# Up-projections of a hybrid decoder trunk in pairs of strips, seven block products for eight

## The chip, the cores and the metric

The kernel runs on one core of one Trainium2 chip. Its time is the device time of one execution in microseconds (us). A core has TensorE (PE, the matrix engine, whose weight loads are listed as PEld), VectorE (DVE), ScalarE (ACT), GpSimd (POOL) and SyncE (SP, which issues the DMAs here). Each takes its instructions in an order fixed when the program is built, and waits on semaphores for the others.

## The reference, cut to what matters

A trunk of two layers on 528 tokens (512 and 16 learned ones ahead) of 1024 channels. Layer 0 mixes tokens with a gated delta net, layer 1 with a short gated convolution; each mixer is followed by a gated FFN, and each of the four sub-layers ends in a layer norm. The change lies in the second, third and fourth sub-layer:

```python
def short_conv_mixer(h, w_in, conv_w, w_out):
    b_gate, c_gate, xv = jnp.split(h @ w_in, 3, axis=-1)     # w_in 1024 x 3072
    u = causal_dwconv(c_gate * xv, conv_w)
    return (b_gate * u) @ w_out

def conv_ffn(h, w_up, conv_w, w_down):
    u, gate = jnp.split(h @ w_up, 2, axis=-1)                # w_up 1024 x 5632
    u = causal_dwconv(u, conv_w)                             # width 3
    return (jax.nn.silu(u) * gate) @ w_down                  # w_down 2816 x 1024

# per layer: h <- layer_norm(ALPHA * h + mixer(h)); h <- layer_norm(ALPHA * h + conv_ffn(h))
```

## The kernel before, in words

Activations lie with channels on the 128 partitions: `h` is [128, 8 blocks of channels, 528 tokens] in fp32. Every product is made in three matmuls with operands split in a high and a low part: `split` (L71 to L73) lets ACT write the high part (L72) and DVE the rest, `lo = src - hi` (L73). `hh` and `hl` are the parts of `h`, `gh` and `gl` those of the gated middle, `whi` and `wlo` those of a weight strip. A strip is the weights of 128 output channels, [128, 8 blocks, 128], 512 KB.

`mm_steps` (L169) runs over the blocks k of a strip and issues high x high (L174), high x low (L175) and low x high (L176) into one PSUM bank. `prep` (L137) loads a strip on SP's queue into one of four raw buffers and splits it; `get` (L153) keeps up to five strips prepared ahead, in ten buffers of a strip each (NW, L129; four of them in the delta net).

The delta net comes first; then for each sub-layer `up` (L688) and `down` (L636). [...] It begins with a lead of six strips whose first halves all go before any second half, so that PE has work while the norm of the second half of the tokens is still being made. `emit` takes the bank: for u a copy on ACT, three taps on DVE (`conv3`, L724), Silu on ACT; for a gate a product on DVE and a split into `gh` and `gl` (`gated`, L732). The FFN's 22 strips of the middle go in groups of 8, 8 and 6 (THIRDS, L103), and after each group `down` adds its part of the second product to `h` (L651, L653). The last `down` of a sub-layer holds back the second halves of five or seven strips, makes the norm of the first half (`lnorm`, L592) beside them, then theirs.

What stands in which order on an engine is decided when the program is built, by a scheduler that goes by its own costs; the code's order is its priority. The banks of `up` and `down` are six (`pm`).

## Time and profile before

| what | us |
|---|---|
| time, median of 3 runs (lowest, highest) | 1389.57 (1387.96, 1390.41) |
| the profiled execution: span from first to last instruction | 1386.2 |
| delta net | 0 to about 378 |
| its output projection and first norms | 378 to about 422 |
| first FFN | 422 to about 805 |
| short convolution | 805 to about 990 |
| second FFN, with the end | 990 to 1386 |
| HBM read and written over the span | 112.05 MB and 2.10 MB, 82 GB/s |

The stages are told apart by where the means of the norms are computed (two each, at 414, 795, 983 and 1354 us for the first of them). Rows of a timeline give start and length in us, then engine, line and operation, output and inputs, shapes and how many were merged; the bracket at the end is the idle time of that engine just before, and what ended it. A row of the groups gives busy us and mean ns of one, then the idle time before it.

### The profile page before, as it was taken

To read this page: it belongs to the slowest core of one execution; us is meant where nothing else is said; L and a number is where in the kernel's file an instruction comes from. 1 tells how busy PE (TensorE), PEld (TensorE's weight loads), DVE (VectorE), ACT (ScalarE), POOL (GpSimd) and SP (SyncE) were. 2 spreads that over 40 slices of the span, in tenths; PEclk is the share of its full clock that TensorE was granted. 3 is DMA by queue.
4 is the path that set the end of the run, shared out by engine and by line. 5 is a ranking of instruction groups with operands and counts; after the bars stand their busy time and mean duration, and the time that the engine had idled before them with its cause. 6 is when DMAs were issued, how large, how long until landed. Compare 5 with 4: busy or idle time off the path is not lost.

```text
span 1386.2 us, 25494 instructions
## 1 busy us (share of the span) xinstructions
PE 1350.4 (97%) x10769; PEld 1288.0 (93%) x10769; DVE 804.9 (58%) x1360; ACT 606.2 (44%) x1218; POOL 90.1 (7%) x132
## 2 busy tenths in 40 slices
PE   8999999999999999999999999999999999999996
PEld 7888998988899999999999999999999889988996
DVE  6767767766469754455344496444775434443436
ACT  6677777676446532233223274222463223322314
POOL 0323322221000000000000000000000000000000
PEclk9999999999999999999999999999999999999999
DMA  5211111211272433233322233333124333322101
GB/s 193 66 58 32 47 32 31 62 32 35 74 244 77 123 93 93 92 94 94 95 79 80 61 107 122 92 92 92 51 87 138 93 97 99 92 92 80 58 1 61
DMA packets 34929, 115.78 MB, mean 84 GB/s; under 512 B 3840, under 2 KB 6400, under 8 KB 34816
## 3 DMA queue, kind: packets, MB, share of 16 engines
q1 hardware_dynamic: 34176, 112.04, 26.3%
q0 software_dynamic: 640, 2.12, 0.4%
q8 instruction: 84, 1.38, 0.4%
q14 instruction: 29, 0.24, 0.1%
HBM read 112.05 MB, written 2.10 MB: 82 GB/s over the span
## 4 chain that ended last, share of the span: by engine, by line
PE 87%; DVE 5%; ACT 4%; issue 2%; POOL 1%; DMA 0%; SPq 0%; ACTq 0%; POOLq 0%; DVEq 0%
PE pu L174 15%; PE pu L175 15%; PE pu L176 15%; PE pd L175 8%; PE pd L174 8%; PE pd L176 8%; PE ps L175 2%; PE ps L174 2%; PE ps L176 2%; DVE acc L316 1%; DVE wlo L73 1%; PE psz L176 1%; PE psz L175 1%; PE psz L174 1%; PE p L403 1%
## 5 line engine op out<-in xcount | busy, mean ns | idle before, releaser
L174 PE MATMUL pu<-hh,whi 128*128 128x258 f32 (+3 forms) x1632 | 477.6, 294 | 1.4 <-ACT hh L632 1.4
L175 PE MATMUL pu<-hl,whi 128*128 128x258 f32 (+3 forms) x1632 | 478.3, 293 | 0.0
L176 PE MATMUL pu<-hh,wlo 128*128 128x258 f32 (+3 forms) x1632 | 477.2, 293 | 0.0
L72 ACT ACTIVATE whi<-raw 128x1024 fp32r<-128x1024 f32 (+2 forms) x209 | 216.7, 1040 | 387.8 <-PE pu L175 168.1
L73 DVE TENSOR_TENSOR wlo<-raw,whi 128x1024 fp32r<-128x1024 f32 (+2 forms) x209 | 249.6, 1196 | 227.0 <-ACT whi L72 224.3
L174 PEld LDWEIGHTS pu<-hh,whi 128*128 128x128 f32 x1632 | 306.8, 188 | 9.1 <-ACT hh L632 1.8
L175 PEld LDWEIGHTS pu<-hl,whi 128*128 128x128 f32 x1632 | 307.3, 188 | 7.5 <-DVE hl L633 0.2
L176 PEld LDWEIGHTS pu<-hh,wlo 128*128 128x128 f32 x1632 | 307.6, 189 | 7.0
L174 PE MATMUL pd<-gh,whi 128*128 128x256 f32 (+3 forms) x704 | 213.4, 303 | 0.0
L175 PE MATMUL pd<-gl,whi 128*128 128x256 f32 (+3 forms) x704 | 212.9, 302 | 0.0
L176 PE MATMUL pd<-gh,wlo 128*128 128x256 f32 (+3 forms) x704 | 212.7, 302 | 0.0
L174 PEld LDWEIGHTS pd<-gh,whi 128*128 128x128 f32 x704 | 132.8, 189 | 5.8
L175 PEld LDWEIGHTS pd<-gl,whi 128*128 128x128 f32 x704 | 132.6, 188 | 5.8
L176 PEld LDWEIGHTS pd<-gh,wlo 128*128 128x128 f32 x704 | 132.7, 188 | 5.7
L174 PE MATMUL ps<-hh,whi 128*128 128x264 f32 x384 | 114.1, 298 | 2.1 <-ACT acc L313 2.1
L176 PE MATMUL ps<-hh,wlo 128*128 128x264 f32 x384 | 115.1, 300 | 0.0
L175 PE MATMUL ps<-hl,whi 128*128 128x264 f32 x384 | 114.6, 298 | 0.0
L174 PEld LDWEIGHTS ps<-hh,whi 128*128 128x128 f32 x384 | 73.4, 191 | 2.6 <-ACT acc L313 2.5
L756 ACT ACTIVATE c<-c 128x516 f32<-128x516 f32 (+1 forms) x44 | 27.6, 632 | 106.8 <-DVE c L727 106.8
L175 PEld LDWEIGHTS ps<-hl,whi 128*128 128x128 f32 x384 | 73.4, 191 | 0.4
L176 PEld LDWEIGHTS ps<-hh,wlo 128*128 128x128 f32 x384 | 73.3, 191 | 0.2 <-DVE wlo L73 0.2
L316 DVE SCALAR_TENSOR_TENSOR acc<-cb,par_sb,acc 128x528 f32<-128x528 f32 x72 | 59.0, 820 | 20.0 <-ACT acc L313 19.6
(228 smaller groups left out, 1865.1 us busy)
## 6 DMA issues: line engine op xcount, KB each, us to landing
raw<-in_w_up_dram SPq DMA_DIRECT2D x88, 512.0 KB, 3.6
raw<-in_w_dn_dram SPq DMA_DIRECT2D x32, 512.0 KB, 3.5
raw<-in_w_bi_dram SPq DMA_DIRECT2D x24, 512.0 KB, 3.6
raw<-in_w_qkv_dram SPq DMA_DIRECT2D x23, 512.0 KB, 3.7
raw<-in_w_dn_dram SPq DMA_DIRECT2D x16, 384.0 KB, 3.1
raw<-in_w_z_dram SPq DMA_DIRECT2D x8, 512.0 KB, 3.6
raw<-in_w_ao_dram SPq DMA_DIRECT2D x8, 512.0 KB, 3.6
raw<-in_w_bo_dram SPq DMA_DIRECT2D x8, 512.0 KB, 3.5
```

What stands on the lines that cost most here:

```text
L72: S.activation(hi, src, AF.Copy)
L73: V.tensor_tensor(lo, src, hi.bitcast(F32), ALU.subtract)
L174: TE.matmul(ps, hi[:, k, :], r_h, start=start and k == 0, stop=False)
L175: TE.matmul(ps, hi[:, k, :], r_l, start=False, stop=False)
L176: TE.matmul(ps, lo[:, k, :], r_h, start=False, stop=stop and k == nk - 1)
L316: V.scalar_tensor_tensor(acc, cb[:, t_ : t_ + T], par_sb[:, wo + t_ : wo + t_ + 1], acc, ALU.mult, ALU.add)
L403: TE.matmul(p1[:CH, c, :CH], N16[:, c, :], r_, start=True, stop=True)
L756: S.activation(c, c, AF.Silu)
```

## The change

Two strips and both halves of the tokens make a 2 x 2 block product: the two strips are cut at half of the channels (A11, A12 of the first, A21, A22 of the second), the tokens likewise in channels and at half of the tokens. Instead of eight block products of four blocks k each there are seven, by the scheme of Strassen in Winograd's form: four weight sums (S1 = A21 + A22, S2 = S1 + A11, S3 = A21 + A11, S4 = S2 + A12, signs put into the token sums and into negated taps), and four token sums made once for a sub-layer (`sums_a`, `sums_b`). In the code a product is called by its weight block. A product has 4 x 3 matmuls of n = 260 columns (first FFN) or 258; a pair has 84 matmuls.

The FFN's groups become 4, 6, 6 and 6: the first is made as before (eight strips, the first six as the lead), the other 18 pairs of gate and u strip as pairs. The short convolution makes two columns of strips as before, then a `down` of two blocks, then eight pairs, and a `down` of six. Weights lie in a ring of 32 + 24 blocks for high and low parts (`room`, `done`) instead of ten strips; `pump` loads and splits what fits, also at the very start. `conv3` of a pair makes its first tap on ACT.

```diff
+GROUPS = ((0, 4), (4, 6), (10, 6), (16, 6))
+SC_GROUPS = ((0, 2), (2, 6))
+PREP = ("A11", "S1", "S2", "A12", "S3", "A22", "S4")
-    THIRDS = ((0, 8), (8, 8), (16, 6))
...
+    SEG = (32, 24)
+    def room(n):
+        g_, p_ = state["seg"], state["pos"]
+        if p_ + n > SEG[g_]:
+            g_, p_ = (g_ + 1) % len(segs), 0
+        for u in live:
+            if u.seg == g_ and u.pos < p_ + n and p_ < u.pos + u.n:
+                return None
...
+    def sums(job, what):
+        a, b = job.raws
+        a11, a12, a21, a22 = a[:, 0:4, :], a[:, 4:8, :], b[:, 0:4, :], b[:, 4:8, :]
+        if what == "S1":
+            job.s = pools[-1].tile([P, 4, P], F32, name=f"s{job.n}", tag="s", bufs=1)
+            V.tensor_tensor(job.s, a21, a22, ALU.add)
+        elif what == "S2":
+            V.tensor_tensor(job.s, job.s, a11, ALU.add)
+        elif what == "S3":
+            V.tensor_tensor(a21, a21, a11, ALU.add)
+        elif what == "S4":
+            V.tensor_tensor(job.s, job.s, a12, ALU.add)
...
+    def pump(end=None):
+        while True:
+            i = state["load"]
+            if i < len(jobs) and i < (n_gdn + 4 if len(pools) == 1 else len(jobs)) \
+                    and state["held"] + len(jobs[i].srcs) <= 2 * len(pools):
+                jobs[i].n = i
+                load(jobs[i])
+                state["load"] += 1
+                continue
+            i = state["prep"]
+            if i >= state["load"] or (end is not None and i >= end):
+                return
+            if not prep_step(jobs[i]):
+                return
...
-    prep(0)
+    pump(1)
     for k in range(1, KD):
         nc.sync.dma_start(h[:, k, :], xt[:, k, :])
...
+    def sums_a(sb):
+        n, B = blocks(sb)
+        for q in (0, 2):
+            ks = slice(q, q + 2)
+            t3 = tmp("c", f"t3_{sb}_{state['use']}_{q}")[:, : 2 * n].rearrange("p (k t) -> p k t", k=2)
+            V.tensor_tensor(t3, B(h, 1, 1)[:, ks], B(h, 0, 1)[:, ks], ALU.subtract)
+            V.scalar_tensor_tensor(sc[:, ks, :n], t3, -1.0, B(h, 0, 0)[:, ks], ALU.mult, ALU.subtract)
+            split(sumh[:, 1, ks, :n], suml[:, 1, ks, :n], sc[:, ks, :n])
+            split(sumh[:, 2, ks, :n], suml[:, 2, ks, :n], t3)
+        for q in (0, 2):
...
+            V.tensor_tensor(t1, B(h, 0, 0)[:, ks], B(h, 0, 1)[:, ks], ALU.subtract)
+            split(sumh[:, 0, ks, :n], suml[:, 0, ks, :n], t1)
+    def sums_b(sb):
...
+            V.scalar_tensor_tensor(sc[:, ks, :n], sc[:, ks, :n], -1.0, B(h, 1, 0)[:, ks], ALU.mult, ALU.subtract)
+            split(B(hh, 0, 1)[:, ks], B(hl, 0, 1)[:, ks], sc[:, ks, :n])
+    def pairs(keys, sb, emit):
...
+        def step(p, what):
+            e1, u3 = sc[:, 0, :n], sc[:, 1, :n]
+            if what == "A11":
+                p.x = bank(f"px{p.nm}")
+                product(p, what, p.x, True, False)
+                S.activation(e1, p.x[:, :n], AF.Copy)
+            elif what == "S1":
+                p.z = bank(f"pz{p.nm}")
+                product(p, what, p.z, True, False)
+            elif what == "S2":
+                product(p, what, p.x, False, what == "A22")
+                S.activation(p.u2, p.x[:, :n], AF.Copy)
+            elif what == "A12":
+                q = bank(f"pq{p.nm}")
+                product(p, what, q, True, True)
+                p.g = tmp("u", f"pg{p.nm}")
+                V.tensor_tensor(p.g[:, :n], e1, q[:, :n], ALU.add)
+            elif what == "S3":
+                product(p, what, p.x, False, what == "A22")
+                S.activation(u3, p.x[:, :n], AF.Copy)
+                p.u = tmp("u", f"pu{p.nm}")
+                V.tensor_tensor(p.u[:, n : 2 * n], u3, p.z[:, :n], ALU.add)
+            elif what == "A22":
+                product(p, what, p.x, False, what == "A22")
+                S.activation(p.u[:, :n], p.x[:, :n], AF.Copy)
+                emit(p.key, 1, p.u)
+            else:
+                product(p, what, p.z, False, True)
+                V.tensor_tensor(p.g[:, n : 2 * n], p.u2, p.z[:, :n], ALU.add)
+                emit(p.key, 0, p.g)
...
+            seq = [(p, "A11"), (p, "S1"), (old, "A22"), (p, "S2"), (p, "A12"), (old, "S4"), (p, "S3")]
...
+            def emit_pair(j, which, t_):
+                if which:
+                    c = cs[j] = tmp("c", f"c{idx}_{k0 + j}")[:, :ng]
+                    conv3(c, t_[:, su - sb :], ng, tap(j), True, S)
+                    S.activation(c, c, AF.Silu)
+                else:
+                    c = cs.pop(j)
+                    V.tensor_tensor(c, c, t_[:, s1 - sb : s1 - sb + ng], ALU.mult)
+                    split(gh[:, j, :ng], gl[:, j, :ng], c)
...
-            up(order(nk, 2, lead), (su, s1), emit, FFN_GRP if lead else ())
+            if lead:
+                up(lead, (su, s1), emit, FFN_GRP, lambda: sums_a(sb))
+                sums_b(sb)
+            else:
+                pairs(range(nk), sb, emit_pair)
             down(idx, nk, gh, gl, s1, s1, first=k0 == 0, final=k0 + nk == KF, last=last)
```

How the change moves instructions shows in three places. The first is DVE's queue in the middle of the first FFN. Before, this is what it does for one u strip and one gate strip (strip 11 of the middle): taps, two gate products, low part, and two low parts of weights.

```order
L725 TENSOR_SCALAR c1_11_7614<-u1_11_7586,par_sb_70 128x516
L727 SCALAR_TENSOR_TENSOR c1_11_7614<-u1_11_7586,par_sb_70,c1_11_7614 128x516 x2
L734 TENSOR_TENSOR c1_11_7614<-c1_11_7614,pu72_7_0_7625 128x258
L734 TENSOR_TENSOR c1_11_7614<-c1_11_7614,pu72_7_1_7650 128x258
L73 TENSOR_TENSOR wlo81_7929<-raw81_7927,whi81_7928 128x1024
L73 TENSOR_TENSOR gl_5088<-c1_11_7614,gh_5087 128x516
L73 TENSOR_TENSOR wlo82_7993<-raw82_7991,whi82_7992 128x1024
```

Now, in the same place, these rows follow each other (L942, L935 and L930 are additions out of PSUM, L210 to L216 weight sums, L988 the gate's product); the taps of strip 12 stand right behind them.

```order
L942 TENSOR_TENSOR pg73_7845<-sc_5027,pz73_7786 128x260
L89 TENSOR_TENSOR wl0_83<-s74_7872,wh0_82 128x512
L988 TENSOR_TENSOR c1_12_7939<-c1_12_7939,pg73_7845 128x516
L210 TENSOR_TENSOR s75_7999<-raw87_7868 128x512
L935 TENSOR_TENSOR pu74_8021<-sc_5027,pz74_7913 128x260
L89 TENSOR_TENSOR gl_5024<-c1_12_7939,gh_5023 128x516
L89 TENSOR_TENSOR wl0_83<-s75_7999,wh0_82 128x512
L214 TENSOR_TENSOR raw87_7868<-raw87_7868,raw86_7866 128x512
L212 TENSOR_TENSOR s75_7999<-s75_7999,raw86_7866 128x512
```

Eight instructions for a pair of strips became eighteen, and emission and preparation of different pairs lie between each other.

The second place is DVE's queue where the first FFN's lead ends. Before, `gl` of strip 3 stands behind weights only, and the first `down` is four strips of the middle away.

```order
L73 TENSOR_TENSOR wlo55_6349<-raw55_6347,whi55_6348 128x1024
L73 TENSOR_TENSOR wlo56_6413<-raw56_6411,whi56_6412 128x1024
L734 TENSOR_TENSOR c1_3_6040<-c1_3_6040,pu48_7_1_6194 128x258
L73 TENSOR_TENSOR wlo57_6473<-raw57_6471,whi57_6472 128x1024
L73 TENSOR_TENSOR gl_5088<-c1_3_6040,gh_5087 128x516
```

Now `gl` of strip 3 is the last block that the first `down` needs, and a token sum (L883) and a pair's preparation stand ahead of it.

```order
L851 TENSOR_TENSOR c1_3_5964<-c1_3_5964,pu48_7_1_6153 128x258
L883 SCALAR_TENSOR_TENSOR sc_5027<-sc_5027,h_67 128x520
L89 TENSOR_TENSOR wl1_5016<-raw56_6051,wh1_5015 128x512
L89 TENSOR_TENSOR wl0_83<-raw56_6051,wh0_82 128x512
L210 TENSOR_TENSOR s56_6065<-raw57_6053 128x512
L89 TENSOR_TENSOR gl_5024<-c1_3_5964,gh_5023 128x516
```

The third place is SP's queue at the start of the program, where `h` is loaded in eight blocks. Before:

```order
L88 DMA h<-in_xt_dram 128x528
L146 DMA raw_86<-in_w_qkv_dram 128x512 x2
L184 DMA h<-in_xt_dram 128x528 x7
L186 DMA par_sb<-in_par_dram 128x333
L187 DMA cst_sb<-in_cst_dram 128x384
```

Now two further strips stand among the blocks of `h`, the second of them into the buffer of the first strip of all:

```order
L106 DMA h<-in_xt_dram 128x528
L199 DMA raw_88<-in_w_qkv_dram 128x512 x2
L199 DMA raw_91<-in_w_qkv_dram 128x1024
L282 DMA h<-in_xt_dram 128x528 x2
L199 DMA raw_97<-in_w_qkv_dram 128x1024
L282 DMA h<-in_xt_dram 128x528 x5
```

ACT and DVE split these strips in the same order, ahead of the later blocks of `h`.

## The prediction

> **What bounds the kernel now.** I read the page first, then a table of stretches, the waits of TensorE, and single rows of the timeline.

> ```profile
> span 1386.2 us, 25494 instructions
> PE 1350.4 (97%) x10769; PEld 1288.0 (93%) x10769; DVE 804.9 (58%) x1360; ACT 606.2 (44%) x1218; POOL 90.1 (7%) x132
> PE 87%; DVE 5%; ACT 4%; issue 2%; POOL 1%; DMA 0%; SPq 0%; ACTq 0%; POOLq 0%; DVEq 0%
> ```

> The page alone would allow a latency-bound kernel, since a busy PE need not be a PE at its peak. The stretches settle it: the first FFN, the short convolution, the second FFN.

> ```profile
> 422.00:805.00 383.00, 383.00 (x3193) 382.32 (x3192) 201.79 (x328) 131.82 (x208) 0.00 (x0) 1.00 0.30 92
> 805.00:990.00 185.00, 183.63 (x1529) 182.96 (x1528) 108.06 (x197) 63.07 (x107) 0.00 (x0) 1.00 0.30 92
> 990.00:1386.00 396.00, 385.39 (x2392) 345.29 (x2390) 205.23 (x328) 136.74 (x227) 0.00 (x0) 1.00 0.27 82
> PE pu L174 <- ACT hh L632: 1.4, 2, 1.0
> ```

> (Columns: PE, PEld, DVE, ACT, POOL, clock, DMA, GB/s.) In the first FFN PE is never idle, DVE is busy 53%; TensorE's waits on other engines in all three are a few microseconds (the row is the largest). So a matmul taken out there comes off the time, until DVE or ACT end later. The clock is 1.00.

> **What goes: matmuls.** How long one takes is the distance between starts, not its printed length, because they overlap:

> ```profile
> 507.65 0.28 PE L174 MATMUL pu<-hh,whi 128*128 128x258 f32 x1
> 510.52 0.28 PE L174 MATMUL pu<-hh,whi 128*128 128x260 f32 x1
> 513.42 0.28 PE L174 MATMUL pu<-hh,whi 128*128 128x258 f32 x1
> 559.87 0.28 PE L174 MATMUL pd<-gh,whi 128*128 128x256 f32 x1
> 561.97 0.28 PE L174 MATMUL pd<-gh,whi 128*128 128x260 f32 x1
> 1096.70 0.39 PE L175 MATMUL pd<-gl,whi 128*128 128x512 f32 x1
> 1101.78 0.39 PE L176 MATMUL pd<-gh,wlo 128*128 128x512 f32 x1
> L174 PE MATMUL pu<-hh,whi 128*128 128x258 f32 x1024 | 288.3, 283 | 1.4 <-ACT hh L632 1.4
> L174 PE MATMUL pu<-hh,whi 128*128 128x256 f32 x272 | 76.3, 281 | 0.0
> L174 PE MATMUL pu<-hh,whi 128*128 128x512 f32 x160 | 62.9, 393 | 0.0
> L174 PE MATMUL pu<-hh,whi 128*128 128x260 f32 x176 | 50.2, 285 | 0.0
> ```

> 24 matmuls of 258 columns lie between the first two rows: 2.87/24 = 0.1196 us. 260: 2.90/24 = 0.1208. 256: 18 in 2.10 = 0.1167. 512: 22 in 5.08 = 0.231, hardly less than two of 256, so narrow moving blocks lose nothing. Each group exists three times (L174 to L176): 3072 of 258, 816 of 256, 480 of 512, 528 of 260. In the changed program's order the up-projections have 720, 240, 48 and 96 of these, and 44 pairs x 84 = 2184 of 258 and 1512 of 260. By width: 258: +168; 256: +576; 512: +432; 260: -1080. The gain is 20.1 + 67.2 + 99.8 - 130.5 = **57 us** (4.1%). The down-projections keep their count and widths.

> **What comes: DVE and ACT work.** Rows for what one instruction costs in a queue that never waits, and alone:

> ```profile
> 379.02 2.52 DVE L73 TENSOR_TENSOR hl<-h,hh 128x518 fp32r<-128x518 f32 x4 [1.12 <-ACT hh L72]
> 804.05 0.74 DVE L653 TENSOR_TENSOR h<-h,pd 128x256 f32<-128x256 f32 x2
> 807.56 1.22 DVE L73 TENSOR_TENSOR wlo<-raw,whi 128x1024 fp32r<-128x1024 f32 x1
> 808.69 0.42 DVE L620 SCALAR_TENSOR_TENSOR r<-s,r 128x260 f32<-128x260 f32 x1
> 599.32 1.55 DVE L727 SCALAR_TENSOR_TENSOR c<-u,par_sb,c 128x516 f32<-128x516 f32 x2
> 828.83 1.28 DVE L625 SCALAR_TENSOR_TENSOR h<-h,par_sb,r 128x256 f32<-128x256 f32 x3
> L73 DVE TENSOR_TENSOR gl<-c,gh 128x512 fp32r<-128x512 f32 x22 | 15.0, 683 | 0.7 <-ACT gh L72 0.7
> 458.92 0.88 DVE L725 TENSOR_SCALAR c<-u,par_sb 128x516 f32<-128x516 f32 x2
> 378.35 2.74 ACT L72 ACTIVATE hh<-h 128x518 fp32r<-128x518 f32 x5
> L752 ACT ACTIVATE u<-pu 128x258 f32<-128x258 f32 x44 | 16.4, 378 | 29.9 <-PE pu L176 29.9
> ```

> Back to back, one starts before its predecessor's printed length is over: (2.52 - 0.68)/3 = 0.61 for about 512 elements, 0.33 out of PSUM, 1.13 for 1024 (807.56 to 808.69). The three-operand forms of 516 I take at 0.68 (0.755 where, as here, one needs the other's result, less the same 0.07), those of 256 at 0.40, tensor_scalar at 0.40. A pair now has on DVE 7 low parts and 4 sums of 512, two of 516 (gate product, low part of gh), three additions out of PSUM, two conv taps: 13 x 0.61 + 3 x 0.33 + 2 x 0.68 = **10.3 us, against 84 x 0.1208 = 10.15 us of PE** (10.05 at 258). ACT has 7 x 0.51 for high parts ((2.74 - 0.7)/4), four copies of 0.38 and three of 516: under 7 us. So in the pair stages DVE, half idle before, comes level with PE. What hides it: the 56-block ring holds two pairs ahead, and a down-projection of six blocks gives PE 288 x 0.119 = 34 us and DVE 16 x 0.33 + 8 x 0.87 (768 elements, between 0.61 and 1.13) = 12. The costs left:

> - Pairs: a full set of preparations falls into 30 of 44 periods, each 0.15 to 0.25 over PE. The tightest bound is a PSUM bank: pz of a pair needs the last addition of the pair two before, two products (2.9 us) after that pair's final product; DVE may lag 2.5 us. So the lag hardly reaches PE: 3 us. Another 4 us for hand-overs ACT to DVE inside a pair, for which no row has the loaded case (bounds: nothing, and 0.5 us a pair, 22).
> - First lead of an FFN. DVE's rows from the first token difference to gh's last low part (t3 to gl of strip 3) are 25 of 0.61, one of 1.13, 11 of 0.68, 0.4 x 5 and 8 x 0.33: 28.5 us.

> ```profile
> 451.13 0.47 DVE L625 SCALAR_TENSOR_TENSOR h<-h,par_sb,r 128x256 f32<-128x256 f32 x1
> 428.85 0.28 PE L174 MATMUL pu<-hh,whi 128*128 128x260 f32 x1
> 834.71 0.88 DVE L633 SCALAR_TENSOR_TENSOR hl<-h,par_sb,hh 128x256 fp32r<-128x256 f32 x2
> 829.91 0.86 PE pu L174 x5
> ```

>   They start at 451.7 and end at 480.2. PE does 384 lead matmuls from 428.85 (0.1202 each) to 475.0 and reaches the fourth block of the down-projection 27 matmuls later, at 478.3: 2 us late, 0.5 more for banks. Before, the group had eight blocks and this was covered. Same order in the second FFN: 5 us together (bounds 0 and 10).
> - Lead of the short convolution. Same count there: 25 x 0.61, 2 x 1.13, 10 x 0.68, 3 x 0.4, 15 x 0.33 = 30.5 us from 835.6 to 866.1; PE, from 829.9 with 240 + 18 matmuls, wants it at 861. The down-projection after it has two blocks, 11.4 us, in which DVE owes 16 updates x 0.40 and about nine of 0.61: again level. 6 us (0 to 12).
> - Pair to down: behind the last product stand copy, tap, two taps, Silu, product, high and low part, by these rows and DVE's order 5.0 us; PE reaches the sixth block after 45 matmuls, 5.4 us. With DVE 1 to 2 us late it is uncovered; five places (at 512 width the cover is 7 us), 5 us (0 to 10).
> - Norms: weights for a lead have 56 blocks instead of 80, so the third to sixth strip are split in the middle of the norm: 1 us at each of three (0 to 3).
> - Start: SP now issues two further 512 KB strips ahead of the rest of h, the second waiting for the first strip's buffer.

> ```profile
> 2.59 3.85 SPq L184 DMA_DIRECT2D h<-in_xt_dram  x7
> 7.61 0.69 DVE L73 TENSOR_TENSOR wlo<-raw,whi 128x512 fp32r<-128x512 f32 x1 [1.27 <-ACT whi L72]
> 10.14 0.42 PE L174 MATMUL ps<-hh,whi 128*128 128x264 f32 x1
> 10.36 0.42 PE L175 MATMUL ps<-hl,whi 128*128 128x264 f32 x1
> 13.79 0.28 PE L174 MATMUL psba<-hh,ba_hi 128*16 128x264 f32 x1
> 13.91 0.28 PE L175 MATMUL ps<-hl,whi 128*128 128x264 f32 x1
> ```

>   That buffer is free at 8.3, so five blocks of h land 3 to 4 us later than before. PE still runs at half pace then (0.22 a matmul of 264, at 13.8 it is 0.12), so part is made up: 1.5 us (0 to 4).

> Sum: 3 + 4 + 5 + 6 + 5 + 3 + 1.5 = 27.5 back of 57: **-29.5 us**. The profiled execution has a span of 1386.2, the median of the runs is 1389.57, so 3.4 lie around it; 1386.2 - 29.5 + 3.4 = **1360**.

> The upper bounds add up to 61 us, more than the gain; the values taken lie nearer to the lower ends, because each walk goes by measured distances and was late by at most 5 us.

> [...]

> **Rivals.**
> 1. DVE keeps up everywhere: only the start and a few microseconds at the leads are paid. For it: every shortfall above but one is under 2.5 us a place. 8 to 10 us back: 1342. Chance 0.22.
> 2. DVE paces the pairs, the slower side. Place: the 30 full periods. If every instruction costs its printed length, a pair takes 13 x 0.69 + 3 x 0.42 + 2 x 0.755 = 11.7. Then 30 x 1.6 = 49, less the 2.5 of slack in seven groups, is 31; the leads' rows grow 14%, 12; with the other 20.5 that is 64 back: **1397**. It decides from 11.5 us a pair on. For it: seven times a pair DVE needs ACT's result first, and it waits for that often now; against it: those are waits of an engine with nothing else to do, and the 0.61 is measured. Chance 0.17.

> ```profile
> DVE wlo L73 <- ACT whi L72: 224.3, 114, 5.1
> ```

> 3. [...] Chance 0.08. [...]

> That the work is not what it says can be left out: the order shows 96 matmuls fewer and 432 of 512 gone.

> **Numbers.** The forecast has 0.53, with a range of its own of 1349 to 1372. With the rivals: 1340 to 1393, the lower end close to a DVE that keeps up, the upper short of a DVE that paces. A measurement here cannot tell less than about 0.2% from no change (1386.8 to 1392.4). Faster 0.83, same 0.05, slower 0.12.

> **What would show it.** Right: 4800 matmuls in the up-projections with distances of 0.12; DVE over 90% busy in pair stages; PE gaps at the lead of the short convolution (about 5 us, released by gh or gl) and at the ends of pair stages, under 0.3 us a pair within. Wrong: PE waiting for wl in every pair, with DVE at 11.5 us or more a period; or gaps of PE at the norms much over 1 us, since preparations there were counted as hidden.

## The result, and the profile after it

The changed kernel takes 1341.61 us (median of 4 runs, 1339.88 to 1343.03) against 1389.66 (4 runs, 1387.96 to 1390.41) beside it: a ratio of 0.9653, 95% interval 0.964 to 0.9667, or 48.0 us less. The forecast of 1360 had the sign and lies on the slow side of it: 29.5 us were expected of the 57 that the matmuls bring, 48.0 came. The time is that of the first rival, 1342. It lies below the forecast's own range of 1349 to 1372 and inside the range with the rivals, 1340 to 1393.

The page of the changed kernel, its head and the chain of waits:

```profile
span 1338.1 us, 26463 instructions
PE 1297.5 (97%) x10673; PEld 1251.8 (94%) x10673; DVE 1059.5 (79%) x1934; ACT 766.2 (57%) x1621; POOL 92.0 (7%) x132
PE 74%; DVE 16%; ACT 4%; issue 2%; DMA 2%; POOL 2%; SPq 0%; ACTq 0%; POOLq 0%; DVEq 0%
```

96 matmuls are gone, DVE is busy 79% instead of 58%, and the chain goes over DVE for 16% instead of 5%. The three stretches again, between the same places of the program (columns as before):

```profile
420.40:781.40 361.00, 359.04 (x2978) 357.54 (x2978) 302.97 (x551) 197.80 (x369) 0.00 (x0) 1.00 0.32 96
781.40:961.10 179.70, 174.99 (x1426) 173.50 (x1424) 157.60 (x309) 94.64 (x189) 0.00 (x0) 0.98 0.30 94
961.10:1338.10 377.00, 365.47 (x2614) 343.45 (x2612) 314.75 (x566) 206.02 (x391) 0.00 (x0) 0.99 0.31 92
```

The first FFN is 22 us shorter, the second 19, the short convolution only 5. Its clock is 0.98, where it was 1.00. TensorE's waits from the first norms to the end (us in total, times, longest; three of 0.7 to 1.0 us at norms are left out) say which places pay:

```profile
PE pd L272 <- DVE bu L851: 3.9, 1, 3.9
PE pd L273 <- DVE gl L89: 1.0, 2, 0.6
PE pd L272 <- DVE h L760: 0.9, 1, 0.9
PE px L272 <- ACT sc L933: 0.5, 1, 0.5
PE pu L274 <- DVE wl L89: 0.3, 1, 0.3
```

In all 44 pairs TensorE waits once, 0.5 us. The rest is in the leads and at their ends, most of it in one wait of the short convolution.

Waits alone leave out slow matmuls, so the next table is worked out from all rows of TensorE's timeline. The stages go from the first mean of one norm to the first mean of the next. "Lost" is by how much the distances between starts exceed the price by width (0.1196 us for 258 columns, in proportion for others, 0.231 for 512).

| stage | before: us, of it lost | after | last version (below) |
|---|---|---|---|
| start to the first mean | 414.5 | 413.0 | 413.1 |
| first FFN | 380.5, 0.9 | 358.5, 3.6 | 356.1, 1.3 |
| short convolution | 188.1, 3.1 | 182.8, 9.8 | 176.4, 3.4 |
| second FFN | 370.9, 1.8 | 351.6, 3.7 | 350.8, 2.9 |
| last norm's two means | 18.0, 1.5 | 18.1, 1.6 | 18.1, 1.6 |
| to the last mean | 1371.9 | 1323.8 | 1314.4 |

From before to after the span up to the last mean falls by 48.1. The start gives 1.5 of it, 11.4 more are lost, and so the matmuls brought 48.1 - 1.5 + 11.4 = 58.0.

The largest loss in rows: first TensorE, then DVE in the same stretch (start, length, engine, line, operands, and in brackets the idle time before), then the clock (the last but two numbers).

```profile
836.03 0.28 PE L274 MATMUL pd<-gh,wl 128*128 128x258 f32 x1
840.20 0.58 PE L272 MATMUL pd<-gh,wh 128*128 128x256 f32 x1 [3.88 <-DVE bu L851]
840.58 0.41 PE L273 MATMUL pd<-gl,wh 128*128 128x256 f32 x1
840.79 0.41 PE L274 MATMUL pd<-gh,wl 128*128 128x256 f32 x1
```

```profile
834.27 1.29 DVE L89 TENSOR_TENSOR wl<-raw,wh 128x512 fp32r<-128x512 f32 x2 [0.48 <-ACT wh L88]
835.48 0.69 DVE L210 TENSOR_TENSOR s<-raw 128x512 f32<-128x512 f32 x1
...
839.12 0.69 DVE L89 TENSOR_TENSOR wl<-raw,wh 128x512 fp32r<-128x512 f32 x1
839.73 0.42 DVE L851 TENSOR_TENSOR bu<-bu,pu 128x256 f32<-128x256 f32 x1
...
841.87 0.69 DVE L89 TENSOR_TENSOR gl<-bu,gh 128x514 fp32r<-128x514 f32 x1
```

```profile
840.00:846.00 6.00, 5.70 (x25) 5.41 (x26) 5.17 (x11) 2.42 (x4) 0.00 (x0) 0.52 0.58 175
846.00:850.00 4.00, 4.00 (x33) 3.81 (x32) 4.00 (x10) 0.63 (x1) 0.00 (x0) 1.00 0.03 6
```

TensorE has run out of work at 836.1, yet the last gate product (L851) stands behind nine weight preparations for the first pairs and is made at 839.73. TensorE waits 3.9 us, then 0.1 for the low part (841.87 + 0.69), and until about 845.6 its matmuls start 0.21 instead of 0.12 us apart, at a granted clock of 0.52 (840 to 846; 1.00 from 846 on): 25 matmuls, some 2.4 us more.

### The profile page after: what moved, and what is told of

Same layout as the page of the kernel before. It is cut to its first block, busy times and chain, and to the rows that moved or that the text cites. A ratio compares the mean times of both kernels' runs of the same rounds, so it can differ in the third digit from the quotient of the medians.

```text
span 1338.1 us, 26463 instructions
## 1 busy us (share of the span) xinstructions
PE 1297.5 (97%) x10673; PEld 1251.8 (94%) x10673; DVE 1059.5 (79%) x1934; ACT 766.2 (57%) x1621; POOL 92.0 (7%) x132
## 4 chain that ended last, share of the span: by engine, by line
PE 74%; DVE 16%; ACT 4%; issue 2%; DMA 2%; POOL 2%; SPq 0%; ACTq 0%; POOLq 0%; DVEq 0%
PE pd L273 8%; PE pd L274 8%; PE pd L272 8%; PE px L272 6%; PE px L274 6%; PE px L273 6%; DVE wl L89 3%; PE pz L272 3%; PE pz L273 3%; PE pz L274 3%; PE ps L274 2%; PE ps L273 2%; PE ps L272 2%; PE pq L272 1%; PE pq L274 1%
## 5 line engine op out<-in xcount | busy, mean ns | idle before, releaser
L88 ACT ACTIVATE wh<-raw 128x512 fp32r<-128x512 f32 (+3 forms) x321 | 238.3, 746 | 199.5 <-PE pd L273 82.5
L89 DVE TENSOR_TENSOR wl<-raw,wh 128x512 fp32r<-128x512 f32 (+3 forms) x321 | 264.9, 835 | 63.4 <-ACT wh L88 62.8
L272 PE MATMUL pd<-gh,wh 128*128 128x256 f32 (+3 forms) x704 | 213.2, 306 | 4.8 <-DVE bu L851 3.9
L273 PE MATMUL pd<-gl,wh 128*128 128x256 f32 (+3 forms) x704 | 214.3, 305 | 1.1 <-DVE gl L89 1.0
L274 PE MATMUL pd<-gh,wl 128*128 128x256 f32 (+3 forms) x704 | 213.3, 303 | 0.0
L272 PEld LDWEIGHTS pd<-gh,wh 128*128 128x128 f32 x704 | 132.6, 190 | 11.1 <-DVE bu L851 4.1
L273 PEld LDWEIGHTS pd<-gl,wh 128*128 128x128 f32 x704 | 133.8, 190 | 7.9 <-DVE gl L89 2.1
L274 PEld LDWEIGHTS pd<-gh,wl 128*128 128x128 f32 x704 | 133.7, 190 | 5.8
L272 PE MATMUL ps<-hh,wh 128*128 128x264 f32 x384 | 114.7, 300 | 0.9 <-ACT acc L411 0.9
L274 PE MATMUL ps<-hh,wl 128*128 128x264 f32 x384 | 115.1, 300 | 0.0
L89 DVE TENSOR_TENSOR wl<-s,wh 128x512 fp32r<-128x512 f32 x132 | 90.7, 687 | 15.0 <-ACT wh L88 12.0
```

Source lines behind the costliest of these rows:

```text
L88: S.activation(hi, src, AF.Copy)
L89: V.tensor_tensor(lo, src, hi.bitcast(F32), ALU.subtract)
L272: TE.matmul(ps, hi[:, k, :], r_h, start=start and k == 0, stop=False, **kw)
L273: TE.matmul(ps, hi[:, k, :], r_l, start=False, stop=False, **kw)
L274: TE.matmul(ps, lo[:, k, :], r_h, start=False, stop=stop and k == nk - 1, **kw)
```

## The experiments

Each is an edit of the changed kernel (1341.6).

**An eighth product.** What is a product worth, and did DVE hold the pairs back?

```diff
                 q = bank(f"pq{p.nm}")
+                mm(q[:, :n], p.job.units[what], 4, *MOV["A11"], 0, 0, n)
                 product(p, what, q, True, True)
```

> Each of the 44 pairs makes one block product more: the weights of A12 times the tokens of A11 go into the bank of A12 ahead of the product that is wanted, which then overwrites them, so the output stays the same. 44 x 12 = 528 matmuls more, 216 of 260 columns at 0.1208 us and 312 of 258 at 0.1196: 26.1 + 37.3 = 63.4 us. Theory A (the pairs of the changed kernel are bound by matmuls alone, as the sum of 0.7 us of TensorE waits in them says): 1341.6 + 63.4 less at most 0.7 = 1404 to 1405, and a count of eight products would make the scheme slower than before. Theory B (the pairs give 7 us back for DVE's lag and its waits for ACT, as the prediction had it): with 1.45 us more of TensorE work a pair those waits vanish, so 1341.6 + 63.4 - 7 = 1398.

1402.49 us (ratio to before 1.0087, 1.0069 to 1.0104), 60.9 more. Up to the last mean, where the spans are free of what varies at the very end, it is 1385.98 against 1323.84: 62.1 for 528 matmuls, 0.118 each. This is close to A and far from B's 56. With eight products the new scheme is slower than the old one, by 0.9%: the gain comes with the product that is left out.

**No weight sums.**

```diff
-        if what == "S1":
-            job.s = pools[-1].tile([P, 4, P], F32, name=f"s{job.n}", tag="s", bufs=1)
-            V.tensor_tensor(job.s, a21, a22, ALU.add)
...
-        own = {"A11": a11, "A12": a12, "A22": a22, "S3": a21}
+        own = {"A11": a11, "A12": a12, "A22": a22, "S3": a21, "S1": a21, "S2": a22, "S4": a12}
```

> The four weight sums of each pair are left out (the products S1 to S4 take raw weight blocks in their place), so the output is not the reference's. DVE loses 4 x 0.61 = 2.4 us a pair, 107 us in all; TensorE's work stays. Theory A (DVE's new work lies beside TensorE's except in the three leads): at most the 0.7 us of waits in pairs and part of the 1.9 and 0.8 us in the FFN leads go, and in the short convolution's lead, where three of the ten instructions ahead of the last gate product are sums, 1.8 of its 3.9 us: 1338 to 1341. Theory B (DVE level with TensorE costs the 7 us of the prediction's lag and hand-overs plus 5 at the edges): 1341.6 - 12 = 1330 or less.

1332.98 us (0.9589, 0.9574 to 0.9603), 8.6 less: between the two theories, and the last mean is 6.7 us sooner. By stage, what is lost falls from 3.6 to 0.9, from 9.8 to 7.0 and from 3.7 to 2.7, 6.5 in all. Only 0.7 of that had been lost in pairs; the rest is at the leads, where A had counted too little. So 107 us of DVE's work taken out are worth 6.7 us: most of it lay beside TensorE's work, but not all. In the short convolution's lead a wait of 2.1 us is left without any sum ahead of it, and slow matmuls behind it.

**More work for DVE**, one, two or four instructions a pair:

```diff
                 emit(p.key, 0, p.g)
+                for _ in range(1):      # 2, 4
+                    V.tensor_tensor(junk, p.g[:, :512], p.g[:, :512], ALU.add)
```

> Behind each pair's gate product DVE adds one block of 512 to itself into a tile that nobody reads: 0.61 us more a pair, 27 us in all; TensorE's work and the output stay. Theory A (what counts is DVE's idle time in a stage of six pairs, 60.7 - 54.5 = 6.2 us, and 6.7 in the eight pairs of the short convolution): 6 x 0.61 = 3.7 a stage is covered, 1341.6 to 1343. Theory B (DVE is level with TensorE, 10.2 against 10.1 us from one gate product to the next in the middle of a stage, so more work shows at once): 1341.6 + 27 = 1368. Theory C (the prediction's slower rival, which decides from 11.5 us a pair): 10.9 a pair, nothing, 1341.6.

> As the run with one added instruction a pair, with two: 1.22 us a pair, 54 us in all. Theory A: 7.3 us a stage against 6.2, and 9.8 against 6.7 in the short convolution, so 1 us at each of six stages and 3 there, less what a lag of up to 2.5 us a stage hides: 1342 to 1351. Theory B: 1341.6 + 54 = 1395. Theory C: 11.5 a pair, just at its limit: 1341.6.

> As the run with one added instruction a pair, with four: 2.44 us a pair, 107 us in all. Theory A: 14.6 - 6.2 = 8.4 us at each of six stages and 19.5 - 6.7 = 12.8 in the short convolution, 63 in all, less 0 to 2.5 of lag in each of seven: 1387 to 1405. Theory B: 1341.6 + 107 = 1449. Theory C: 12.7 a pair, 1.2 over its limit in 30 full periods: 1341.6 + 37 = 1379.

1341.23 us (0.9655, 0.964 to 0.967), 1346.29 (0.9693, 0.9679 to 0.9708) and 1370.42 (0.9863, 0.9848 to 0.9877): -0.4, +4.7 and +28.8 for 27, 54 and 107 us of DVE. B falls at once, and C, which allows nothing up to 11.5 us a pair, had nothing at two and 37 at four. A holds for one and two and gives too much for four, 45 to 63. For one instruction the profile is less kind than the times: its last mean is 2.7 us later than the changed kernel's, about as much as the runs of one kernel scatter. What A rests on is DVE's busy time in a stage of six pairs, first in the changed kernel, then with one more instruction:

```profile
595.09:655.79 60.70, 60.70 (x506) 60.60 (x505) 54.46 (x92) 40.77 (x78) 0.00 (x0) 1.00 0.38 114
595.10:655.80 60.70, 60.70 (x507) 60.70 (x507) 56.23 (x95) 41.01 (x77) 0.00 (x0) 1.00 0.37 107
```

The length is the same to 0.01 us, and DVE fills idle time. With four, TensorE waits mostly where the pairs end (about 12 us of idle time, against 4 inside them); the largest rows, of which the third is the wait in the short convolution's lead that the changed kernel has too:

```profile
PE pd L272 <- DVE pg L943: 4.3, 3, 1.9
PE pd L272 <- ACT gh L88: 4.0, 3, 1.4
PE pd L272 <- DVE bu L852: 3.9, 1, 3.9
PE pd L273 <- DVE gl L89: 2.3, 7, 0.8
```

The three stages of the first FFN lose 14.4 - 2.9 = 11.5 us more, 3.8 each, of 14.6 added: 10.8 are covered, not the 6.2 to 8.7 of A. The scheduler also puts matmuls of the last pair between those of the down-projection in this program, so the added work and the new order are not told apart here.

**The start.** The two further strips again behind all of `h`:

```diff
-                    and state["held"] + len(jobs[i].srcs) <= 2 * len(pools):
+                    and state["held"] + len(jobs[i].srcs) <= 2 * len(pools) and i < state["cap"]:
...
     nc.sync.dma_start(cst_sb, cst)
+    state["cap"] = len(jobs)
     pump(2)
```

> Only the early loads are undone: strips 2 and 3 of the delta net are loaded behind all blocks of h, as before the change. Theory A (the prediction's: the two strips hold h's later blocks back, 1.5 us lost): 1340.1. Theory B (the strips that come early are what lets the delta net end 1.6 us sooner than before, 412.96 against 414.55 at the first norm's mean, though TensorE then waits 2.5 instead of 0.7 us for the second block of h): 1343 or more. Theory C (what is lost at 8 to 16 us and what is won behind it are independent of these loads): 1341.6 within 0.5.

1342.4 us (0.9657, 0.9637 to 0.9677; runs from 1340.2 to 1344.8), not to be told from the changed kernel's time. The place itself can be looked at: the first mean of a norm, before, in the changed kernel and here.

```profile
414.48 0.71 PE L598 MATMUL mean<-acc,onesm 128*128 128x262 f32 x2
```

```profile
412.96 0.71 PE L705 MATMUL mean<-acc,onesm 128*128 128x262 f32 x2
```

```profile
415.09 0.71 PE L706 MATMUL mean<-acc,onesm 128*128 128x262 f32 x2
```

The profiles of the other eight kernels that load early at the start in the same way have it at 412.4 to 413.4. TensorE's second wait at the start is a part of the changed kernel:

```profile
10.13 0.40 PE L272 MATMUL psba<-hh,ba_hi 128*16 128x264 f32 x1 [2.54 <-ACT hh L88]
```

Here it is 0.7 us. By the mean this looks like B, but TensorE's clock falls twice within the delta net here, and in none of the other profiles. Each time it is behind a wait of 1.9 to 2.0 us (two rows of TensorE, then stretches: behind the length stands TensorE's busy time, and the clock is the last but two):

```profile
213.51 0.49 PE L570 MATMUL sa<-vn,kd 106*128 106x128 f32 x2 [1.96 <-ACT vn L567]
292.58 0.50 PE L570 MATMUL sa<-vn,kd 106*128 106x128 f32 x2 [1.89 <-ACT vn L567]
```

```profile
211.01:214.42 3.41, 1.45 (x15) 1.22 (x13) 1.16 (x3) 3.40 (x9) 0.00 (x0) 1.00 0.01 2
214.42:217.83 3.41, 3.41 (x20) 3.40 (x19) 3.27 (x5) 1.76 (x8) 0.10 (x1) 0.50 0.00 0
289.52:292.93 3.41, 1.52 (x14) 1.31 (x12) 0.71 (x2) 3.23 (x7) 0.00 (x0) 1.00 0.00 0
292.93:296.34 3.41, 3.41 (x21) 3.40 (x20) 3.36 (x7) 2.30 (x10) 0.00 (x0) 0.50 0.00 0
```

Two stretches at half clock can cost up to 3.4 us (an estimate: half of 2 x 3.41), more than the 2.1 us between the two means. So it is not shown what the early strips win or lose, and the three theories stay open.

**Holding the pairs' preparation in the short convolution's lead** until the down-projection's first two strips are issued:

```diff
-            if i >= state["load"] or (end is not None and i >= end):
+            if i >= state["load"] or i >= state["hold"] or (end is not None and i >= end):
...
+        state["hold"] = state["use"] + 2 * KD
         up(SC_LEAD, (su, su, s1), emit, SC_GRP, lambda: sums_a(sb))
...
             together(go(0, 0), go(0, 1), go(1, 0))
+            state["hold"] = 10 ** 6
             together(go(1, 1))
```

> In the lead of the short convolution the preparation of the first pairs is held until the down-projection's first two strips are issued; nothing else changes, the work is the same. In the changed kernel the last gate product there stands behind ten preparations: its bank is full at about 836, DVE takes it at 839.73, TensorE waits 3.9 us for it, another 0.9 for the low part, and its next 25 matmuls are 0.215 instead of 0.119 us apart, 2.4 us. Theory A (the order in DVE's queue makes the wait, and the gap makes the slow matmuls): all but about 1 us of the 7.2 goes, 1335 to 1337, the matmuls behind it 0.12 apart. Theory B (the amount of DVE's work in this lead makes it, 30.5 us as the prediction counted): the wait only moves to the first pair's weights or the banks of the down-projection, 1340 to 1342. Theory C (the wait goes, but the slow matmuls have another cause): 1338 to 1339, still 0.215 apart for some 5 us.

1338.96 us (0.9634, 0.9618 to 0.965), 2.65 less, its interval overlapping the changed kernel's; the last mean is 1.3 sooner. The wait for the gate product went, and another came. DVE, then TensorE:

```profile
838.57 0.69 DVE L212 TENSOR_TENSOR s<-s,raw 128x512 f32<-128x512 f32 x1
...
843.39 0.69 DVE L89 TENSOR_TENSOR wl<-s,wh 128x512 fp32r<-128x512 f32 x1
843.99 0.42 DVE L760 SCALAR_TENSOR_TENSOR h<-h,pd 128x258 f32<-128x258 f32 x1
```

```profile
841.13 0.28 PE L274 MATMUL pd<-gh,wl 128*128 128x256 f32 x1
844.46 0.58 PE L272 MATMUL pd<-gh,wh 128*128 128x258 f32 x1 [3.06 <-DVE h L760]
844.84 0.42 PE L273 MATMUL pd<-gl,wh 128*128 128x258 f32 x1
```

Nine preparations in a row now stand ahead of an update of `h` that frees a bank. Slow matmuls (0.22 us from 844.84 to 845.06, where before the gap they are 0.12 apart) follow the gap to its new place, which is against C. Whether B is right or the lump is only in another wrong place is what the next run tells.

**Dripping.** The same hold in all three leads, and then one unit (short convolution) or two (FFN) per strip of the down-projection:

```diff
+            if i >= state["load"] or i >= state["hold"] and not state["drip"] or (end is not None and i >= end):
...
+            state["drip"] -= i >= state["hold"]
...
             for m in range(2, KD):
+                state["drip"] = 1        # 2 in the FFN's branch
                 together(go(m, 0))
                 together(go(m, 1))
+            state["hold"] = 10 ** 6
```

> In the leads of the short convolution and of both FFNs the preparation of pairs is held until the second strip of the down-projection behind the lead; then, per strip of it, one unit (short convolution) or two (FFN) may be prepared, so that DVE's updates of h are never behind a lump. The work is the same. Where the hold alone was tried, the wait for the last gate product went, but nine preparations in a row (838.57 to 843.99) then stood ahead of the next update of h, TensorE waited 3.1 us for that bank, and its next 27 matmuls were 0.215 us apart. Theory A (it is the order in DVE's queue that makes these waits, and a gap that makes the slow matmuls): no gap over 1 us there, no matmuls at 0.215, 5 to 6 of the 7.2 us of the short convolution's lead and 1 to 2 of the 2.7 of the FFNs' go: 1334 to 1337. Theory B (DVE's amount of work between the lead and the first pairs is too much): TensorE waits for the first pairs' weights instead, 1338 to 1341.

1331.97 us (0.9586, 0.9572 to 0.96), 9.6 less than the changed kernel and clear of its interval. From the first FFN's lead to the end of the second FFN these are all of TensorE's waits:

```profile
PE pu L273 <- ACT hh L740: 0.7, 1, 0.7
PE pd L273 <- ACT gh L88: 0.5, 1, 0.5
```

The first of these was there before. Lost time falls by 2.3, 6.4 and 0.8 us in the three stages (table above), with the work unchanged, and no matmuls at 0.21 are left. So A, at a time that is 2 us below its range: it was the order of the work, not its amount. The edit moves ACT's half of each preparation along with DVE's; that the queue that counted was DVE's is read from the rows above, where TensorE waits for DVE and DVE does not stop.

**The short convolution's lead alone, and the start once more.** Two kernels around the dripping version: only its part in the short convolution, and all of it with the two strips loaded behind the first four blocks of `h`.

> The dripping preparation in the lead of the short convolution alone; the leads of the two FFNs are as in the changed kernel. Theory A (each lead's order costs its own time): of the 9.6 us that the three places gave together (1341.6 to 1332.0), the short convolution's 6.4 by its stage in the traces, the FFNs' 2.4 and 0.8 stay: 1335 to 1336, and the two FFN stages as in the changed kernel within 1 us. Theory B (the order of one lead changes what the later stages do): an FFN stage differs by more than 1 us, and the time is off by as much.

> The dripping preparation in all three leads, and at the program's start the two further strips are loaded behind the first four blocks of h instead of among the first two. Theory A (the second wait at the start, 2.5 us for the second block of h, is lost time that the early strips alone make; the strips are wanted only from about 20 us on): the first norm's mean comes 0.5 to 2.5 us sooner than 413.1, the time is 1329.5 to 1331.5. Theory B (what is won behind the start hangs on strips that come as early as they do; all blocks of h are in use only later): the mean comes later, up to 415.1, and the time is 1332 to 1334.

1332.91 us (0.9596, 0.9583 to 0.9609) and 1331.57 (0.9584, 0.957 to 0.9598). The first is 0.9 behind the full version where 3.2 were expected; at the last mean it is 1.7 (1316.13 against 1314.43). The short convolution has its whole gain (182.8 to 176.3 us), and the FFN stages are as in the changed kernel within 0.9, which is A's mechanism; the FFNs' part is about half of what was expected, and the time is 2 us below A's range. The second moves the first mean from 413.1 to 412.2 and the time by 0.4. This is in the direction of A, but not more than the runs scatter, and stays open.

The dripping version, with or without the other start, is the fastest of all: 57 us under the kernel before.

## Why the prediction had the sign and the mechanism, and gave back too much

- **What bounds, and what goes.** TensorE did bound each stage, and the matmuls' 57 us came: 58.0 by the stages, 0.118 us each by the eighth product.
- **DVE's period.** 10.3 us a pair were worked out. The gate product (L988) of two pairs in the middle of a stage, between which DVE is never idle:

```profile
527.17 0.69 DVE L988 TENSOR_TENSOR c<-c,pg 128x516 f32<-128x516 f32 x1
...
537.39 0.69 DVE L988 TENSOR_TENSOR c<-c,pg 128x516 f32<-128x516 f32 x1
```

  10.22 us against TensorE's 10.15. The distances of 0.61 hold under full load, shorter than the printed lengths of 0.69: a low part of weights (L89) starts at 526.56, the gate product at 527.17, the next weight sum (L210) at 527.78.
- **Pairs, 3 + 4 us: measured 0.7.** A stage was judged by its tightest period. But DVE needs to be level only there: over the six pairs of a stage it is idle for 60.70 - 54.46 = 6.2 us. In the down-projection ahead of it, where weights of the first pairs are prepared too, it is busy 22.8 of 34.2 us:

```profile
560.85:595.09 34.24, 34.24 (x290) 34.24 (x289) 22.82 (x42) 9.98 (x16) 0.00 (x0) 1.00 0.27 87
```

  Two added instructions a pair cost 4.7 us; one costs nothing that the times can tell.
- **Pair to down, 5 us: no wait at any of the places.** The cover was worked out rightly and then not believed. One of the places, DVE's last low part and TensorE's matmul that wants it:

```profile
660.62 0.68 DVE L89 TENSOR_TENSOR gl<-c,gh 128x516 fp32r<-128x516 f32 x1
```

```profile
661.17 0.28 PE L272 MATMUL pd<-gh,wh 128*128 128x260 f32 x1
661.35 0.39 PE L273 MATMUL pd<-gl,wh 128*128 128x260 f32 x1
```

  `gl` is done at 661.30, TensorE comes at 661.29 and loses less than 0.2. "With DVE 1 to 2 us late it is uncovered" was the condition, and DVE was not late. With four added instructions it is, and these are the places that wait.
- **Norms, 3 us: measured 0.5 at most.** In the three norms ahead of a lead the stretches between the two means are 19.7, 22.2 and 21.1 us, where they were 19.7, 22.0 and 20.7; splitting strips there is hidden.
- **Start, 1.5 us lost: the first mean comes 1.5 sooner.** The wait was foreseen, and it measures 2.5 us; what makes up for it within the delta net no run shows.
- **FFN leads, 5 us: about 4.** The two stages lose 2.7 and 1.9 more than before, 0.7 of it in a pair; the dripping takes 2.3 and 0.8 of it away.
- **Lead of the short convolution, 6 us: 6.7**, right in size and place, but the amount of DVE's work was named as its cause, and the runs show the order: the same work in another order leaves 0.3. The size is partly luck, because 2.4 of the 6.7 are slow matmuls, which the forecast's sum does not have.
- **Third rival.** Matmuls at half pace behind a gap stand in one place of the changed kernel's three stretches: behind the wait of 3.88 us, where the granted clock is 0.52, and they are 2.4 of these 6.7 us. The other waits there are 1.0 us or less, and the clock behind them is 1.00.
- **Second rival.** DVE does not pace the pairs. The point from which it would was put at 11.5 us a pair; by the times costs begin between 10.8 (nothing) and 11.4 (4.7 us), so this was nearly right.

The step that failed is the sum of the costs left. For pairs, edges, norms and start it took 16.5 us, from values between nothing and a bound. For the pairs' lag and the edges the walk had found a cover that was just enough; for the hand-overs in the pairs, the norms and the start it had no row that gave the price. Measured, these four come to 0.7 + 0 + 0.5 - 1.5, or nothing. The three leads, where the walk had found no cover, had 11 and measured 10.6. Had only the places without cover been charged, the forecast would have been 57 - 11 = 46 less, and 48.0 came; that it comes so near is partly luck, since the 1.5 us of the start are in the 48.0 and nothing here explains them.

## What to carry to other kernels

When work is moved onto an idle engine, compare its busy time with the length of a whole stage, with what it can do ahead in the stage before, and not the tightest period alone. Charge those places where the walk finds no cover; here the others came to nothing. Where an engine carries both preparations and the last link to the bottleneck's next work, keep preparations out of the queue ahead of that link and let them in a few at a time: here that order was worth 9.6 us at unchanged work, about all that the change had given back (57 - 48.0 = 9.0).

## What the runs showed of the hardware

Some gaps in TensorE's work had a price behind them. Eight gaps of 2.1 to 4.9 us in these profiles (3.88 in the changed kernel, 3.06 in the run with the hold, 2.1 without the weight sums), all in the short convolution's lead or the down-projection behind it, were each followed by 3.5 to 6.6 us in which matmuls started 0.21 us apart; after eight gaps of 1.0 to 1.9 us ahead of products, behind the first norms, they were 0.12 apart again after two or three. The longest of the harmless ones, in the run with four added instructions a pair:

```profile
573.37 0.38 PE L272 MATMUL pd<-gh,wh 128*128 128x256 f32 x1 [1.93 <-DVE pg L943]
573.59 0.28 PE L273 MATMUL pd<-gl,wh 128*128 128x256 f32 x1
```

The length of a gap does not decide alone: in the run with the start undone, waits of 1.96 and 1.89 us in the delta net did cost the clock, 0.50 in the stretches behind them (rows in that section).

```profile
290.14:293.55 3.41, 1.62 (x17) 1.41 (x16) 0.71 (x2) 2.80 (x6) 0.00 (x0) 1.00 0.00 0
571.94:575.36 3.42, 1.99 (x16) 1.96 (x17) 3.42 (x7) 1.27 (x2) 0.00 (x0) 1.00 0.60 205
```

So it matters how a gap falls on these stretches, which differs from profile to profile. This is read from the records; no run was made to test it.

At the very end, behind a wait of 1.0 us, the same 16 matmuls of the last variance take 3.7 or 5.4 us from profile to profile. Here they are in the changed kernel and in the run with the hold, each with the clock over their time:

```profile
1325.56 3.72 PE L713 MATMUL var<-s,onesm 128*128 128x256 f32 x16 [1.02 <-ACT s L712]
1325.56:1329.28 3.72, 3.72 (x16) 2.94 (x16) 1.76 (x6) 2.67 (x7) 0.00 (x0) 1.00 0.01 2
```

```profile
1324.24 5.41 PE L713 MATMUL var<-s,onesm 128*128 128x256 f32 x16 [1.02 <-ACT s L712]
1324.24:1329.65 5.41, 5.41 (x16) 4.14 (x16) 1.76 (x6) 2.67 (x7) 0.00 (x0) 0.68 0.00 0
```

The work is identical, the granted clock is not: 1.00 against 0.68. These 1.7 us are why places were compared by the last mean; how much of the 3 us and more by which runs of one kernel differ comes from the clock is not shown.
